# A two-layer Conformer trunk on one core: values product of the attention as two split passes, with a written matmul order, weight remainders by adding DMA and the residual parked in DRAM

## The chip, the cores and the metric

The kernel runs on one core of a Trainium2 chip. The metric is the device time of one execution in microseconds (us). Engines are named as the profile names them: PE is the matrix engine (PEld its weight loads), DVE the vector engine, ACT the activation engine, POOL the general engine, SP the engine that issues most DMAs.

## The reference

The input is 512 frames of 1024 channels; 16 learned meta tokens are put in front, which makes 528 tokens. Two layers follow, each with a feed-forward block (SwiGLU, 2816 wide, added at half weight), a mixer, and a second feed-forward block. A final norm drops the meta tokens.

The mixer normalises the stream to `u` and makes one combined projection into q, k, v (512 wide each), a convolution's value `a` and gate `b` (512 each), and two output gates `gs` and `gc` (1024 each). Branch A is stick-breaking attention, 8 heads of 64 channels: with z = q·k/8, the weight of an earlier token s for token t is sigmoid(z_ts) times the product of 1 − sigmoid(z_tj) over the tokens j between them. In logarithms that is a softplus, a running sum over the keys and an exponential. Branch B is a gated causal convolution of 31 taps, a LayerNorm and a swish. Each branch goes through a projection to 1024 (`ao`, `co`), is multiplied by the sigmoid of its gate, and their sum goes through `wo` and is added to the stream.

## The kernel before

**Number format.** The matrices are fp32. A fast pass of the PE takes operands in a shortened form (fp32r), so each factor is split into a rounded part `hi` and a remainder `lo`, and a product is three passes: hi·hi, hi·lo, lo·hi. `split` (L71) does it with an ACT copy (L73, the rounded part) and a DVE subtraction (L74, the remainder). Activations lie with channels on the partitions and tokens along the free dimension; in the last layer's mixer and second feed-forward block only the 512 frames are computed (mode `XO`), before that all 528 tokens (mode `FULL`, two halves of 264 columns).

**Weights.** `units` (L124) lists every weight tile in the order of use. For the mixer a unit is a 128 x 1024 tile (512 KB), for one output block of 128 channels. `fetch` (L171) brings raw tiles by DMAs on SP's queue into three buffers (`RAW`); `prep_unit` (L205) splits a raw tile into `wh` and `wl`, of which there are four buffers each; `unit` (L230) prepares up to `LOOK` = 3 units ahead of the one handed out. In the feed-forward blocks some sums of weight tiles are made by DMAs that add into SBUF, issued by POOL (`fetch_sums`, L202).

**The mixer** (L644) runs in stages. First the four `b` and `a` units, whose product becomes the convolution's input. Then, for each of four pairs of heads i, the projections q, k, v (`qkv`, L732) and `attend` (L749); some `gs` units follow each pair (`GS_FILL`). The attention of a pair cuts the keys into four blocks (`PIECES`, L642) with 256, 272, 400 and 512 query columns. For each block: scores q·k into PSUM (L816, L817) and the causal mask (L819); a softplus of three ACT passes and one DVE pass (L743); a split (L829); the running sums as products with triangular and all-ones matrices (L833 to L836); an exponential on ACT into `a` (L839); the values product (L843). That last product is in plain fp32, for each head on 64 of the array's 128 columns, the two heads' outputs on the two halves of one PSUM bank. An extra small fp32 product (L809) brings in the 16 last keys. After all keys `po` is split into `oh` and `ol` (L845).

The last stage (L857 on) multiplies the attention's output by `ao`, makes the eight `gc` units, ends the convolution (`conv_some`, L680, which otherwise puts four taps behind each evacuation on DVE), normalises it (`chan_sum` on POOL, L878; `rstd_from`, L902), multiplies by `co`, then `wo`, and adds to the residual `h`.

**Order.** A list scheduler puts each engine's instructions into a fixed order when the kernel is built, by priority. `attend` runs at raised priority and its values products at lowered priority (`priority(EARLY)`), so the attention's matmuls are strewn among the projections'. PSUM holds three `ps` banks for projections, two `z` tiles of two banks and one `po` bank during the attention.

Of the kernel before, what the change touches and what calls it, by code (L numbers as in the profile page):

```python
# [7 lines left out]
F32 = mybir.dt.float32  # L8
# [5 lines left out]
P = 128  # L14
# [20 lines left out]
GS_FILL = ((0,), (1,), (2,3), (4,5, 6, 7))  # L35
NEG = -1e30

# [18 lines left out]
def kernel(ctx, tc, hT, par, const, wg1, wu1, wd1, win, wao, wco, wout, wg2, wu2, wd2, out):  # L56
# [8 lines left out]
    spool = ctx.enter_context(tc.tile_pool(name="spool", bufs=1))  # L65

# [58 lines left out]
    for l in range(DEPTH):  # L125
        for fi, (wg, wu, wd) in enumerate(((wg1, wu1, wd1), (wg2, wu2, wd2))):
            if fi == 1:
                for i in range(4):
                    units += [(("b", l, i), win[l, 16 + i], 8), (("a", l, i), win[l, 12 + i], 8)]
                for i in range(4):  # L130
                    units += [(("q", l, i), win[l, i], 8), (("k", l, i), win[l, 4 + i], 8), (("v", l, i), win[l, 8 + i], 8)]
                    if i:
                        units += [(("gs", l, j), win[l, 20 + j], 8) for j in GS_FILL[i - 1]]
                units += [(("gs", l, j), win[l, 20 + j], 8) for j in GS_FILL[3]]
                units += [(("ao", l, jj), wao[l, jj], 8) for jj in range(4)]
                units += [(("gc", l, j), win[l, 28 + j], 8) for j in range(8)]
                units += [(("co", l, jj), wco[l, jj], 8) for jj in range(4)]
                units += [(("wo", l, j), wout[l, j], 8) for j in ORDER]
# [66 lines left out]
    def prep_unit():  # L205
# [47 lines left out]
    h = [hpool.tile([P, T], F32, name=f"h{k}") for k in range(KD)]  # L253
# [390 lines left out]
    def mixer(l, st, omode, after):  # L644
        last = omode == XO
        with ExitStack() as es:
            bp = es.enter_context(tc.tile_pool(name=f"mix{l}", bufs=1, reuse_waits="tile"))
            u = st["u"]
            rs = {}
            halves = {FULL: (slice(0, HALF), slice(HALF, T)), XO: (slice(META, T),)}  # L650
# [17 lines left out]
            def times(dst, outs, other, d0=0, taps=CONV_STEP):  # L668
# [3 lines left out]
                conv_some(taps, i)  # L672
# [24 lines left out]
            def project(psp, *key, mode=FULL):  # L697
                return gemm_b(psp, unit(*key), 0, KD, u, mode)

            with tc.tile_pool(name=f"psm{l}", bufs=3, space=bass.MemoryType.PSUM, reuse_waits="tile") as psp, \  # L700
# [6 lines left out]
                with tc.tile_pool(name=f"glu{l}", bufs=1, reuse_waits="tile") as glu:  # L707
                    for i in range(4):
                        outs = project(None, "b", l, i)
# [8 lines left out]
                        times(c, project(psp, "a", l, i), rs["r"], PAD)  # L718
# [3 lines left out]
                gates = []  # L722

                def gate_sb(j):
                    g = spool.tile([P, T], F32, tag="sa", bufs=8, name=f"gs{j}")
                    times(g, project(psp, "gs", l, j, mode=omode), rs["r"])
                    gates.append(g)

                o_parts = []
                with tc.tile_pool(name=f"att{l}", bufs=1, reuse_waits="tile") as ap_:  # L730

                    def qkv(i):  # L732
                        ts = []
                        for nm, s, mode in (("q", 0.125, omode), ("k", 1.0, FULL), ("v", 1.0, FULL)):
                            t = spool.tile([P, T], F32, tag="sb", bufs=4, name=nm + "f")
                            for ps, c in project(psp, nm, l, i, mode=mode):
                                ev = dve.scalar_tensor_tensor(out=t[:, c], in0=ps, scalar=s, in1=rs["r"][:, c],  # L737
                                                              op0=ALU.mult, op1=ALU.mult)
                            conv_some(CONV_STEP, ev)
                            ts.append(t)  # L740
                        return ts
# [7 lines left out]
                    def attend(i, qf, kf, vf):  # L749
                        QS, KH, KL = [], [], []  # L750
                        qc = META if last else 0
                        for hh in range(2):
                            r = slice(64 * hh, 64 * hh + 64)
                            o = slice(64 - 64 * hh, 128 - 64 * hh)
                            qs = ap_.tile([P, T], F32R, tag=f"qs{hh}", bufs=1, name="qs")
                            kh = ap_.tile([P, SEQ], F32R, tag=f"kh{hh}", bufs=1, name="kh")
                            kl = ap_.tile([P, SEQ], F32R, tag=f"kl{hh}", bufs=1, name="kl")
                            act.copy(qs[r, qc:], qf[r, qc:])
                            act.copy(kh[r], kf[r, :SEQ])
                            act.copy(kh[o], kf[r, :SEQ])  # L760
                            dve.tensor_tensor(out=qs[o, qc:], in0=qf[r, qc:], in1=f(qs[r, qc:]), op=ALU.subtract)
                            dve.tensor_tensor(out=kl[r], in0=kf[r, :SEQ], in1=f(kh[r]), op=ALU.subtract)
                            dve.tensor_tensor(out=kl[o], in0=kf[r, :SEQ], in1=f(kh[r]), op=ALU.subtract)
# [7 lines left out]
                        zs = ztile()[:, 0, :]  # L771
# [9 lines left out]
                        pe.matmul(zs[:, :w], l4[:, 0:P], e4[:, :w], start=False, stop=True, skip_group_check=True)  # L781
                        pe.matmul(zs[:, 32:48], l4[:, P:2 * P], e4[:, :16], start=True, stop=True, skip_group_check=True)
                        fn(a4[:, :w], zs[:64, :w], AF.Exp, bias=bias[:64, 3:4])
                        corner = ap_.tile([P, 2, 16], F32, tag="corner", bufs=2, name="corner")
                        zc = zs[96:128, 0:64].rearrange("p (a b) -> p a b", a=2)[:, :, :16]
                        dve.tensor_copy(corner[96:128], zc)

                        pt = psp.tile([P, 512], F32, tag="ps", name="pt")
                        for t in range(4):
                            pe.transpose(pt[:, t * P:(t + 1) * P], vf[:, t * P:(t + 1) * P], ident)  # L790
                        v = ap_.tile([P, 4, P], F32, tag="v", bufs=2, name="v")
                        dve.tensor_copy(v.rearrange("p t c -> p (t c)"), pt)
                        vb = ap_.tile([64, 2, P], F32, tag="vb", bufs=2, name="vb")
                        pool.memset(vb, 0.0)
                        pt = psp.tile([P, 512], F32, tag="ps", name="pt2")
                        pe.transpose(pt[:16, :P], vf[:, SEQ:T], ident)
                        for hh in range(2):
                            c = slice(64 * hh, 64 * hh + 64)
                            act.copy(vb[32 * hh:32 * hh + 16, 0, c], pt[:16, c])
                            if not last:  # L800
                                act.copy(vb[32 * hh:32 * hh + 16, 1, c], v[:16, 0, c])
                        oh = bp.tile([P, T], F32R, tag=f"oh{i}", bufs=1, name="oh")
                        ol = bp.tile([P, T], F32R, tag=f"ol{i}", bufs=1, name="ol")
                        if not last:
                            pe.matmul(zs[:, 64:80], vb[:, 1, :], a4[:, 16:32], start=True, stop=True, skip_group_check=True)
                            act.copy(oh[:, :META], zs[:, 64:80])
                            dve.tensor_tensor(out=ol[:, :META], in0=zs[:, 64:80], in1=f(oh[:, :META]), op=ALU.subtract)
                        po = psz.tile([P, 512], F32, tag="o", bufs=1, name="po")
                        pe.matmul(po[:, 496:512], vb[:, 0, :], a4[:, :16], start=True, stop=False, skip_group_check=True)  # L809
                        later = []  # L810
                        for t, q0, n, m0 in PIECES:
# [9 lines left out]
                            zz = z[:, :, :n]  # L821
                            sp = ap_.tile([P, 2, 512], F32, tag="big", bufs=4, name="sp")[:, :, :n]
# [184 lines left out]
```

## Time and profile before

| | us |
|---|---|
| median of 3 runs (2201.63 to 2203.7) | 2202.39 |
| the profiled execution, its own time | 2201.58 |
| span of the profiled execution, first to last instruction | 2199.8 |
| PE busy | 2181.2 |
| DVE busy | 1616.1 |
| ACT busy | 1034.7 |
| POOL busy | 386.2 |

Busy time is the union of an engine's instruction times, so overlapping matmuls count once. A matmul's recorded duration contains its way through the array, in which the next one already runs: what one matmul costs is the distance to the next start. The two mixers take about 369 to 753 us and 1470 to 1842 us of the span; the rest is feed-forward.

### The profile page before, as it was taken

How to read it: one execution, taken by the hardware profiler on the slowest of the kernel's cores; microseconds unless marked ns; L12 is line 12 of the kernel's file. 1: busy time of each engine (PE TensorE's matmuls, PEld its weight loads, DVE VectorE, ACT ScalarE, POOL GpSimd, SP SyncE). 2: the span in 40 equal slices, each digit the busy share in tenths (PEclk: the TensorE clock that was granted, in tenths of full speed). 3: DMA queues.
4: the chain of work that ended last, by engine and by line, in shares of the span. 5: the costliest groups of instructions: out<-in, count | busy, mean ns of one | idle time of the engine just before them, and what ended most of it. 6: DMA issues, size and time to landing. Idle time of an engine off the chain costs nothing.

```text
span 2199.8 us, 39441 instructions
## 1 busy us (share of the span) xinstructions
PE 2181.2 (99%) x16210; PEld 2060.7 (94%) x16210; DVE 1616.1 (73%) x2152; ACT 1034.7 (47%) x1454; POOL 386.2 (18%) x321
## 2 busy tenths in 40 slices
PE   9999999999999999999999999999999999999998
PEld 9999999988899999999999999999777788999897
DVE  7867686877787767676877676868777787776685
ACT  6434355366525435343554343553665265344354
POOL 1322310000000122313113223101000001312220
PEclk9999999999999999999999999999999999999999
DMA  8465443211122456464365654432111225575532
GB/s 232 140 158 142 127 116 106 87 49 52 55 87 87 135 135 172 139 164 122 97 168 151 162 141 129 115 106 87 56 41 68 86 96 139 155 181 139 154 105 78
DMA packets 120580, 261.68 MB, mean 119 GB/s; under 512 B 13392, under 2 KB 17488, under 8 KB 120400
## 3 DMA queue, kind: packets, MB, share of 16 engines
q1 hardware_dynamic: 97248, 217.70, 30.1%
q0 software_dynamic: 22464, 40.90, 11.5%
q8 instruction: 127, 2.08, 0.4%
q10 hardware_dynamic: 688, 0.55, 0.1%
q14 instruction: 53, 0.43, 0.1%
HBM read 257.01 MB, written 2.10 MB: 118 GB/s over the span
## 4 chain that ended last, share of the span: by engine, by line
PE 97%; DVE 1%; ACT 1%; issue 0%; POOL 0%; DMA 0%; POOLq 0%; DVEq 0%; ACTq 0%
PE ps L664 25%; PE ps L547 15%; PE pb L547 15%; PE ps L246 11%; PE pb L246 6%; PE pe L246 6%; PE pe L547 5%; PE z L664 2%; PE ps L474 2%; PE po L843 2%; PE pe L474 1%; PE z L833 1%; PE pb L474 1%; PE ps L521 1%; PE z L816 1%; PE z L835 1%
## 5 line engine op out<-in xcount | busy, mean ns | idle before, releaser
L73 ACT CAST wh<-wr 128x1024 fp32r<-128x1024 f32 (+4 forms) x379 | 352.5, 932 | 591.9 <-PE ps L664 168.3
L74 DVE TENSOR_TENSOR wl<-wr,wh 128x1024 fp32r<-128x1024 f32 (+4 forms) x379 | 438.7, 1159 | 71.9 <-ACT wh L73 66.4
L73 ACT CAST wh<-s 128x1024 fp32r<-128x1024 f32 x158 | 165.8, 1049 | 275.9 <-DVE s L223 91.3
L74 DVE TENSOR_TENSOR wl<-s,wh 128x1024 fp32r<-128x1024 f32 x158 | 215.9, 1366 | 59.5 <-ACT wh L73 58.8
L607 POOL TENSOR_TENSOR h<-h,dt 128x528 f32<-128x528 f32 (+1 forms) x96 | 179.2, 1872 | 261.2 <-DVE dt L605 258.4
L664 PE MATMUL ps<-uh,wh 128*128 128x264 f32 (+1 forms) x864 | 220.5, 312 | 0.3 <-DVE kf L737 0.3
L664 PE MATMUL ps<-uh,wl 128*128 128x264 f32 (+1 forms) x864 | 214.5, 308 | 0.0
L664 PE MATMUL ps<-ul,wh 128*128 128x264 f32 (+1 forms) x864 | 213.9, 307 | 0.0
L202 POOL DMA_DIRECT2D s<-wg x78 | 73.0, 945 | 746.2 <-DMA s<-wg 261.2
L692 DVE SCALAR_TENSOR_TENSOR y<-uc,prm,y 128x528 f32<-128x528 f32 (+1 forms) x240 | 181.4, 756 | 4.7
L547 PE MATMUL ps<-ul,wh 128*128 128x264 f32 (+1 forms) x624 | 177.3, 284 | 0.0
L547 PE MATMUL pb<-sl,wh 128*128 128x264 f32 (+1 forms) x624 | 176.9, 283 | 0.0
L547 PE MATMUL ps<-uh,wl 128*128 128x264 f32 (+1 forms) x624 | 176.8, 283 | 0.0
L547 PE MATMUL pb<-sh,wl 128*128 128x264 f32 (+1 forms) x624 | 176.8, 283 | 0.0
L547 PE MATMUL pb<-sh,wh 128*128 128x264 f32 (+1 forms) x624 | 176.5, 283 | 0.0
L547 PE MATMUL ps<-uh,wh 128*128 128x264 f32 (+1 forms) x624 | 176.1, 282 | 0.0
L664 PEld LDWEIGHTS ps<-uh,wh 128*128 128x128 f32 x864 | 143.2, 188 | 20.4 <-issue 10.7
L664 PEld LDWEIGHTS ps<-uh,wl 128*128 128x128 f32 x864 | 141.6, 188 | 13.4 <-issue 7.2
L664 PEld LDWEIGHTS ps<-ul,wh 128*128 128x128 f32 x864 | 142.0, 188 | 12.5 <-issue 6.6
L246 PE MATMUL ps<-al,wh 128*128 128x264 f32 (+1 forms) x616 | 142.4, 301 | 0.5 <-DVE al L74 0.2
L246 PE MATMUL ps<-ah,wh 128*128 128x264 f32 (+1 forms) x616 | 141.8, 300 | 0.0
L246 PE MATMUL ps<-ah,wl 128*128 128x264 f32 (+1 forms) x616 | 141.7, 300 | 0.0
(291 smaller groups left out, 5985.3 us busy)
## 6 DMA issues: line engine op xcount, KB each, us to landing
wr<-wd SPq DMA_DIRECT2D x96, 384.0 KB, 3.5
wr<-win SPq DMA_DIRECT2D x72, 512.0 KB, 3.2
wr<-wg SPq DMA_DIRECT2D x117, 256.0 KB, 3.0
wr<-wu SPq DMA_DIRECT2D x117, 256.0 KB, 3.4
s<-wg SPq DMA_DIRECT2D x78, 256.0 KB, 4.6
s<-wu SPq DMA_DIRECT2D x78, 256.0 KB, 5.9
s<-wg POOLq DMA_DIRECT2D x78, 256.0 KB, 5.2
s<-wu POOLq DMA_DIRECT2D x78, 256.0 KB, 7.1
```

Of the source, the lines that this page charges most:

```text
L73: act.copy(hi, x)
L74: dve.tensor_tensor(out=lo, in0=x, in1=f(hi), op=ALU.subtract)
L202: pool.dma_start(t[:, a:b], src, accum_op=ALU.add)
L246: pe.matmul(ps[:, c, :n], wt[:, k0 + k, :], xt[:, s:s + n], start=(k == 0 and pi == 0), stop=(k == nk - 1 and pi == 2))
L474: pe.matmul(ps[:, e, :TH], wt[:, k, :], xt[:, s], start=(k == ORDER[0] and pi == 0), stop=(k == ORDER[-1] and pi == 2))
L521: pe.matmul(ps[:, e, :TH], wt[:, k, :], xt[:, s], start=(k == 0 and pi == 0), stop=(k == KD - 1 and pi == 2))
L547: pe.matmul(ps[:, e, :TH], wt[:, 4 * e + kk, :], xt, start=start and kk == 0 and pi == 0, stop=kk == 3 and pi == 2, skip_group_check=True)
L607: pool.tensor_tensor(out=tri(h[j], mode), in0=tri(h[j], mode), in1=tri(t, mode), op=ALU.add)
L664: pe.matmul(ps, wt[:, k0 + k, :], xt[:, s], start=(n == 0 and pi == 0), stop=(n == nk - 1 and pi == 2))
L692: t = dve.scalar_tensor_tensor(out=y, in0=uc[i][:, c0 + k:k + T], scalar=col(w0 + k), in1=y, op0=ALU.mult, op1=ALU.add)
L816: pe.matmul(z[:, hh, :n], KH[hh][:, ks], qq, start=True, stop=False, skip_group_check=True)
L843: pe.matmul(po[c, q0 - META:q0 - META + n], v[:, t, c], a[:, hh, :], start=False, stop=(t == 0), skip_group_check=True)
```

## The change

- The values product: `a` is split into `ah` and `al`; the values of the two heads are laid out as [hi of head 0, lo of head 0, lo of head 1, hi of head 1], so that for one head the stationary tile is 128 columns wide and holds its hi and lo side by side. Two fp32r passes (`ah`, `al`) give the hi part and the lo part of the output on different halves of the partitions. `po` grows from one bank to two. `end` adds the halves: ACT copies of both, a DVE subtraction per head, and one DVE addition over the pair. The small product of the 16 last keys is issued once per head.
- The order: within the attention PE's instructions stand in the order in which the program writes them (`manual_schedule`). `attend` becomes a generator that yields nine or ten times per pair; at each yield half a projection (`by_halves`, one half of the tokens, or half the channels in mode XO) is issued. `products` lists q, k, v, gs and now four of the gc units for that. The tail of a pair (running sums of the longest block, the last values products, the end) is issued in three steps within the next pair. `ps` falls from three banks to two.
- Weights of the mixer: ACT writes `hi`, then ACT writes `−raw` into `lo` (which rounds to −hi), and a DMA issued by POOL adds the raw tile from DRAM a second time. The DVE subtraction is gone for these units.
- The residual: `h` is written to a DRAM tile by eight DMAs on SP at the mixer's start and read back by eight at the start of its last stage. In between its space holds qs, kh, kl and the temporary `ot`; `big` tiles go from four to six.
- The last stage: four gc units have moved ahead into the attention, `ao` stands after the convolution's sums, and `chan_sum` runs on DVE. The convolution takes two taps (three in mode XO) behind each half.

```diff
-GS_FILL = ((0,), (1,), (2,3), (4,5, 6, 7))
+GS_FILL = ((0, 1), (2, 3), (4, 5), (6, 7))
+GC_FILL = 4
+BIG = 6
+MIXER = ("b", "a", "q", "k", "v", "gs", "ao", "gc", "co", "wo")
...
-            split(raw[:, :nk], hi[:, :nk], lo[:, :nk])
+            if key[0] in MIXER:
+                act.copy(hi[:, :nk], raw[:, :nk])
+                act.activation(lo[:, :nk], raw[:, :nk], AF.Copy, scale=-1.0)
+                pool.dma_start(lo[:, :nk], src[:, :nk].bitcast(F32R), accum_op=ALU.add)
+            else:
+                split(raw[:, :nk], hi[:, :nk], lo[:, :nk])
...
+            keep = dram.tile([KD, P, T], F32, tag="keep", bufs=1, name="keep")
+            for k in ORDER:
+                nc.sync.dma_start(keep[k], h[k])
...
+                        v = ap_.tile([P, 4, 4, 64], F32R, tag="v", bufs=2, name="v")
+                        act.copy(v[:, :, 0:4:3], ptv)
+                        dve.tensor_tensor(out=v[:, :, 1:3], in0=ptv, in1=f(v[:, :, 0:4:3]), op=ALU.subtract)
...
-                                    pe.matmul(po[c, q0 - META:q0 - META + n], v[:, t, c], a[:, hh, :], start=False,
-                                              stop=(t == 0), skip_group_check=True)
+                            split(a, ah, al)
...
+                        def values(t):
+                            ah, al, q0, n = acts.pop(t)
+                            for hh in range(2):
+                                for p in (ah, al):
+                                    pe.matmul(po[:, hh, q0 - META:q0 - META + n], v[:, t, hh * P:hh * P + P], p[:, hh, :],
+                                              start=False, stop=(t == 0 and p is al), skip_group_check=True)
...
+                        def end():
+                            values(0)
+                            ot = hold(6, SEQ, "ot")
+                            for hh in range(2):
+                                r, o = (slice(64 * e, 64 * e + 64) for e in (hh, 1 - hh))
+                                act.copy(oh[r, META:], po[r, hh, :])
+                                act.copy(ot[r], po[o, hh, :])
+                                dve.tensor_tensor(out=ol[r, META:], in0=po[r, hh, :], in1=f(oh[r, META:]), op=ALU.subtract)
+                            dve.tensor_tensor(out=ol[:, META:], in0=f(ol[:, META:]), in1=f(ot), op=ALU.add)
+                        ends.extend((end, lambda: values(1), lambda: sums_and_weights(0)))
...
+                    with tc.manual_schedule(engines={mybir.EngineType.PE}):
+                        for i in range(4):
+                            for _ in attend(i, step, *parts(i)):
+                                next(beside, None)
...
+                for k in ORDER:
+                    h[k] = hpool.tile([P, T], F32, tag=f"h{k}", bufs=1, name=f"h{k}")
+                    nc.sync.dma_start(h[k], keep[k])
```

The order of a pair, as `attend` writes it ("|" is a yield, at which half a projection is issued): transposes of v and the corner product | running sums of the previous pair's longest block | its values(1) and scores(3) | its values(0) and end, small products | scores(2) | sums(3) | scores(1) | values(3), sums(2) | sums(1), scores(0) | values(2) |. The numbers are key blocks; block 3 has 256 query columns, block 0 has 512.

## Rows read from the trace of the kernel before

**Rows 1.** The page: the span, the busy time of PE, and the shares of the chain of waits by engine; then the head of the chain's own view, its shares by line.
```profile
span 2199.8 us, 39441 instructions
PE 2181.2 (99%) x16210; PEld 2060.7 (94%) x16210; DVE 1616.1 (73%) x2152; ACT 1034.7 (47%) x1454; POOL 386.2 (18%) x321
...
PE 97%; DVE 1%; ACT 1%; issue 0%; POOL 0%; DMA 0%; POOLq 0%; DVEq 0%; ACTq 0%
...
by line: PE ps L664 25.1%; PE ps L547 15.4%; PE pb L547 14.9%; PE ps L246 10.5%; PE pb L246 5.6%; PE pe L246 5.6%; PE pe L547 5.2%; PE z L664 2.2%; PE ps L474 2.1%; PE po L843 1.8%; PE pe L474 1.3%; PE z L833 1.2%; PE pb L474 1.1%; PE ps L5
```
**Rows 2.** Stretches of the span: attention (with the begin of the last stage) and the rest of the last stage of the first mixer. Columns: busy us of each engine with the number of instructions, granted clock, DMA share, GB/s.
```profile
404.00:665.00 261.00, 259.75 (x1908) 231.66 (x1907) 201.09 (x299) 132.43 (x192) 12.42 (x12) 1.00 0.19 63
665.00:753.00 88.00, 88.00 (x721) 87.94 (x720) 69.90 (x115) 50.45 (x73) 0.00 (x0) 1.00 0.27 90
```
**Rows 3.** The chain of waits in order of time (start us, us, what): one projection of 48 matmuls of 264 columns, and a run of 144 matmuls of 512 columns.
```profile
375.32 5.84 PE ps L664 x48
...
1707.06 33.45 PE ps L664 x144
```
**Rows 4.** PE's instructions in order of time, first mixer, around one values product (start us, us to the last end, line, operation, count).
```profile
448.91 0.28 PE L664 MATMUL ps<-ul,wh 128*128 128x264 f32 x1
449.12 0.65 PE L843 MATMUL po<-a,v 128*64 128x256 f32 x2
449.70 0.50 PE L816 MATMUL z<-qs,kh 128*128 128x512 f32 x1
450.03 0.39 PE L817 MATMUL z<-qs,kl 128*128 128x512 f32 x1
```
**Rows 5.** The same view of the second mixer, where the products of both heads stand together.
```profile
1578.22 1.08 PE L843 MATMUL po<-a,v 128*64 128x512 f32 x4
1579.23 0.51 PE L664 MATMUL ps<-uh,wh 128*128 128x512 f32 x1
```
**Rows 6.** Groups of PE's instructions by line and shape (count, busy us, mean ns of one, idle before).
```profile
L843 PE MATMUL po<-a,v 128*64 128x512 f32 x32 | 11.8, 618 | 0.0
L835 PE MATMUL z<-sh,trir 128*128 128x512 f32 x16 | 6.3, 395 | 0.0
L809 PE MATMUL po<-a,vb 64*128 64x16 f32 x16 | 3.0, 264 | 0.2 <-DVE ol L74 0.2
```
**Rows 7.** Groups on ACT and DVE in the first mixer's attention (404 to 665 us), by shape.
```profile
L73 ACT CAST wh<-wr 128x1024 fp32r<-128x1024 f32 x32 | 33.5, 1048 | 68.8 <-PE ps L664 60.7 <-PE z L664 5.1 <-issue 2.8
L97 ACT ACTIVATE sp<-sp,bias 128x800 f32<-128x800 f32 x8 | 7.7, 965 | 0.2
L744 ACT ACTIVATE sp<-z 128x800 f32<-128x800 f32 x4 | 3.3, 831 | 0.0
L73 ACT CAST sh<-sp 128x800 fp32r<-128x800 f32 x4 | 3.4, 859 | 1.4 <-DVE sp L747 1.4
L73 ACT CAST oh<-po 128x512 fp32r<-128x512 f32 x4 | 2.3, 585 | 2.3 <-PE po L843 2.3
...
L692 DVE SCALAR_TENSOR_TENSOR y<-uc,prm,y 128x528 f32<-128x528 f32 x109 | 83.3, 764 | 2.0
L74 DVE TENSOR_TENSOR wl<-wr,wh 128x1024 fp32r<-128x1024 f32 x31 | 41.7, 1345 | 1.1 <-ACT wh L73 0.8
L670 DVE TENSOR_TENSOR gs<-ps,rstd 128x264 f32<-128x264 f32 x16 | 6.4, 428 | 12.5 <-PE ps L664 12.5
L747 DVE SCALAR_TENSOR_TENSOR sp<-z,sp 128x800 f32<-128x800 f32 x4 | 3.9, 986 | 2.9 <-ACT sp L97 2.9
L74 DVE TENSOR_TENSOR sl<-sp,sh 128x800 fp32r<-128x800 f32 x4 | 4.0, 989 | 0.1
L74 DVE TENSOR_TENSOR ol<-po,oh 128x512 fp32r<-128x512 f32 x4 | 2.8, 692 | 3.4 <-ACT oh L73 3.4
```
**Rows 8.** Groups over the whole span: the split of a block's scores, all sizes together (rounded part, remainder).
```profile
L74 DVE TENSOR_TENSOR sl<-sp,sh 128x512 fp32r<-128x512 f32 (+3 forms) x32 | 29.0, 905 | 6.8 <-ACT sh L73 4.4 <-PE po L843 2.1
...
L73 ACT CAST sh<-sp 128x512 fp32r<-128x512 f32 (+3 forms) x32 | 25.4, 794 | 24.4 <-DVE sp L747 13.7 <-DVE sp L827 8.7 <-PE po L843 2.0
```
**Rows 9.** Who waited for whom over the span (total us, times, longest us): ACT's weight copies for a free buffer, and PE's waits in the attention.
```profile
ACT wh L73 <- PE ps L664: 168.3, 64, 6.9
...
PE pt L790 <- DVE vf L737: 2.2, 4, 0.7
```
**Rows 10.** DMA: the queues of SP and of POOL (packets, MB, share of 16 engines); one of the lines that issue on POOL's queue with KB each and median us to landing; POOL's adding DMAs alone, how long POOL was busy with one (ns, min, median, max) and the time to landing.
```profile
q1 hardware_dynamic: 97248, 217.70, 30.1%
q0 software_dynamic: 22464, 40.90, 11.5%
...
s<-wu POOLq DMA_DIRECT2D x78, 256.0 KB, 7.1
...
L202 POOL DMA_DIRECT2D s<-wu x78: 857/1192/2583, 28.8 to 2111.6; - x78
...
DMA to landing us min/median/max: 4.0/5.9/10.5
```
**Rows 11.** DVE in order of time at the end of the first mixer's convolution: from the norm to the first and the last split of its output.
```profile
666.65 0.70 DVE L378 TENSOR_SCALAR nt<-ps_ln 128x528 f32<-128x528 f32 x1
...
674.76 1.33 DVE L74 TENSOR_TENSOR yl<-y,yh 128x528 fp32r<-128x528 f32 x2 [0.53 <-ACT yh L73]
...
678.83 0.70 DVE L74 TENSOR_TENSOR yl<-y,yh 128x528 fp32r<-128x528 f32 x1
```

More of the change, by code (lines that the diff above doesn't have):

```diff
@@ L666, in gemm_b, with by_halves, times @@
                 return outs
-            def times(dst, outs, other, d0=0, taps=CONV_STEP):
+            def by_halves(psp, mode, *key):
+                hi, lo = unit(*key)
+                for s in halves[mode]:
+                    ps = psp.tile([P, 512], F32, tag="ps", name="ps")[:, :s.stop - s.start]
+                    for n, k in enumerate(ORDER):
+                        if n == KD // 2 and len(halves[mode]) == 1:
+                            yield None
+                        xh, xl = u[k]
+                        for pi, (wt, xt) in enumerate(((hi, xh), (hi, xl), (lo, xh))):
+                            pe.matmul(ps, wt[:, k, :], xt[:, s], start=(n == 0 and pi == 0),
+                                      stop=(n == KD - 1 and pi == 2))
+                    yield ps, s
+            def times(dst, outs, other, d0=0):
                 for ps, s in outs:
@@ L803, in attend @@
[L803 to L808, printed above, removed]
@@ L809, in attend @@
-                        pe.matmul(po[:, 496:512], vb[:, 0, :], a4[:, :16], start=True, stop=False, skip_group_check=True)
-                        later = []
-                        for t, q0, n, m0 in PIECES:
+                                act.copy(vb[32 * hh:32 * hh + 16, 2, c], pt[:16, c])
+                        yield
+                        step(0)
+                        if i:
+                            yield
+                        step(1)
+                        later, acts = {}, {}
@@ new lines, in attend @@
+                        dve.tensor_copy(corner[96:128], zc)
+                        scores(*PIECES[0])
+                        yield
+                        step(2)
+                        oh = bp.tile([P, T], F32R, tag=f"oh{i}", bufs=1, name="oh")
+                        ol = bp.tile([P, T], F32R, tag=f"ol{i}", bufs=1, name="ol")
+                        if not last:
+                            pe.matmul(zs[:, 64:80], vb[:, 2, :], a4[:, 16:32], start=True, stop=True, skip_group_check=True)
+                            with priority(-EARLY):
+                                act.copy(oh[:, :META], zs[:, 64:80])
+                                dve.tensor_tensor(out=ol[:, :META], in0=zs[:, 64:80], in1=f(oh[:, :META]),
+                                                  op=ALU.subtract)
@@ new lines, in attend @@
+                        yield
+                        scores(*PIECES[1])
+                        yield
+                        sums_and_weights(3)
+                        yield
+                        scores(*PIECES[2])
+                        yield
+                        po = psz.tile([P, 2, 512], F32, tag="o", bufs=1, name="po")
+                        for hh in range(2):
+                            pe.matmul(po[:, hh, 496:512], vb[:, hh, :], a4[:, :16], start=True, stop=False,
+                                      skip_group_check=True)
```

190 lines of the change are left out of this document (105 added, 85 removed).

## The prediction

> **What bounds the kernel now.** I read the page first: PE is busy for 2181.2 of the 2199.8 us of the span, and the chain of waits gives it 97% [rows 1]. So a change moves the time by what it takes off PE's row of work, or by the waits that it puts into that row. The stretches come next: in the attentions and in the last stage of the mixer PE is busy practically all the time as well, while DVE has 201 of 261 us and ACT 132 [rows 2]. A busy PE is not yet a PE at its pace, because overlapping durations hide small gaps. The pace stands in the chain in order of time: 48 matmuls of 264 columns in 5.84 us and 144 of 512 in 33.45 us, so 122 ns and 232 ns each, 0.455 ns a column [rows 3]. The list of who waited for whom shows no large wait of PE in the attentions; the largest, for the transposes, is 2.2 us in all [rows 9]. What remains is the price of the matmuls themselves, and there the fp32 values product stands out: 1.8% of the span lies on it [rows 1], that is 39.6 us.
>
> The profiled execution took 2201.58 us for a span of 2199.8, so 1.8 us lie around the span, and it is 0.8 us under the median of 2202.39. I make the sum in the trace and give the result against the median. A measurement of this kernel can tell about 0.2% (4.4 us) from no change.
>
> **The values product.** One product of 256 columns is two PE instructions, which hold PE from 449.12 to 449.70 us, 0.58 us [rows 4]; for 512 columns it is 1.01 us [rows 5]. After the change one head of one pair has 256+272+400+512 = 1440 columns in two passes, and there are 16 such heads in the two layers: 46,080 columns. Other fp32r products with the same 512 columns have the duration of the projections [rows 6], so I take 0.455 ns: 21.0 us. Saved: 39.6 − 21.0 = 18.6 us.
>
> The Trainium skill's page "TensorE: Matmul & The Clock Gate" (Part 3, packing small matmuls) says that products whose outputs lie in different column groups of the array run at the same time; the two heads of the old product are such a pair. The trace agrees where they stand next to each other: four instructions of 512 columns end together after 1.01 us [rows 5]. By that rule for all 64 products the old cost would be 24 us and the saving 3 us. The chain's 39.6 us is measured and decides: most of the 64 are not side by side.
>
> **Changing between formats.** Before a product the next start comes after 0.21 instead of 0.12 us (448.79, 448.91, 449.12), and after it the first matmul takes 0.33 instead of 0.23 (449.70, 450.03, 450.26) [rows 4]: 0.19 us for each burst of fp32. With 64 products, some of them neighbours, there are 32 to 64 bursts, 6 to 12 us; I take 56, 10.6 us, because the share on the chain says that most stand alone. This goes wholly, since the new passes have the format of the projections around them.
>
> **The small product of the last keys** is issued twice per pair instead of once: 16 more instructions. The 16 of before are busy 3.0 us [rows 6]. Cost 0 to 3.0 us, taken as 3.0, because short fp32 work doesn't hide behind its neighbours.
>
> So PE's own work falls by 18.6 + 10.6 − 3.0 = 26.2 us. The rest of the change must not hand that back.
>
> **Load of DVE and ACT.** In the first attention's 261 us DVE loses 31 remainders, 41.7 us [rows 7]; it gains 16 remainders of `a` at 0.905 (the price of the same tiles of the scores [rows 8]), 14.5 us, and three subtractions or additions instead of one at a pair's end, 4 x 2 x 0.69 = 5.5 us. That makes 201 − 42 + 20 = 179 us. ACT gains the negated copies (33.5 us as the rounded ones [rows 7]), 16 copies of `a` at 0.794 [rows 8] = 12.7 us, three more copies per pair's end at 0.585 [rows 7] = 7.0 us, and the four copies of v that it takes over at that price, 2.3 us: 132 + 55.5 = 188 us. In a stretch of some 248 us that is 72% and 76%. Neither becomes the bound, so I cost the work at nothing; but in queues so full a waiting chain meets other work.
>
> **The written order.** PE executes in order, so a matmul that waits holds all that follows. The tightest place is block 1 with 400 query columns: after its scores, two half projections (2 x 2.92), values(3) (4 x 0.12) and sums(2) (about 8 x 0.12) are written before sums(1) needs its softplus: 7.3 us. The softplus with its split takes 0.83 + 2 x 0.965 + 0.99 + 0.86 + 0.99 = 5.6 us unhindered [rows 7]. The 1.7 us between are used up by one convolution tap (0.76) and one weight copy (1.05) ahead in the queues [rows 7]. The other blocks have three half projections and more. I charge one such tap, 0.75 us, for each of the eight pairs: 6 us. The bounds are nothing (the cover holds everywhere) and, at the other end, a wait at each of the 39 yields per layer, which is the rival below. PSUM banks for projections fall from three to two: a half takes 2.9 us and its evacuation about 0.43, so DVE may be some 2.5 us late before PE notices; that too is in the 6 us.
>
> **Remainders by adding DMA.** A weight tile's buffers come free when the unit four places earlier ends (ACT's copies wait for exactly that, 168.3 us in all [rows 9]), and the tile is wanted three units later: 3 x 5.84 = 17.5 us in the last stage, more in the attention. Of this ACT takes 2 x 1.05 and POOL about 1.2 for the issue, which leaves some 14 us to land. The adding DMAs of 256 KB landed in 5.2 and 7.1 us (the second of a pair) and 10.5 at most [rows 10]; 512 KB is bounded by 5.2 below and twice 10.5 above, and I take 8, near a pair's 7.1, which is the same bytes. The engines bear it: SP's queue took 30.1% of the span for 217.7 MB, 1.6 us per 512 KB, POOL's 11.5% for 40.9 MB, 3.2 us [rows 10], together 4.8 of 5.84 us per unit in the last stage. I cost it at nothing; its cover is the lead of three units, and if that goes, every late microsecond is one of PE's.
>
> **The residual, the sums, the other moves.** Writing and reading h is 2.2 MB each way, 6.6 us of the DMA engines at SP's rate [rows 10]. On SP's queue the reads stand ahead of later weight fetches and wait for the last pair's end, some 5 us of copies; raw tiles are fetched about three units ahead, so this takes 12 of 17 us of lead and costs nothing by itself. Six channel sums per layer on DVE cost 0.7 us each, in a stage where DVE also loses its remainders. After the norm's matmul the convolution's first output took 8.8 us and its last 12.9 [rows 11]; the two gc units that are left to cover it last 11.7 us, and the first is wanted first. Nothing, at most 2 us per layer. What is late next is then the same row of matmuls.
>
> The sum: 2201.6 − 26.2 + 6 = 2181.4 in the trace, **2182 us** for the median.
>
> **Rivals.**
> *The written order starves PE (slower).* If the queues of ACT and DVE are so ordered that at each of the 78 yields the awaited tile is 0.5 us late, PE stands for 39 us: 2202.4 − 26 + 39 = 2215. It decides from 0.34 us per yield on. For it: both queues above 70%, chains of six hops between the two engines, and two ps banks. Against it: most blocks have 9 us or more of cover for chains of 4 to 7 us. Chance 0.11.
> *Remainders land late (slower).* Were 512 KB to take 15 us instead of 8, each of the 20 or so units of a last stage would be about 1 us late, 40 us in all: 2216. It decides from about 14 us. For it: 83% of the DMA engines in that stage. Against: 10.5 us as the longest of 156. Chance 0.04.
> *The heads already run side by side.* Saving 3 and 32 bursts (6), less 3 and the waits of 6: 2202. Against it stands the chain's 39.6 us. Chance 0.02; with waits that happen to eat the whole gain, 0.07 within 0.2%.
> *The order costs nothing and closes other gaps.* All 64 bursts (12 us) go, and the transposes' waits: 18.6 + 12 + 2 and little for the small products: 2170. Chance 0.13.
> My forecast, 2174 to 2196, has 0.65.
>
> **The numbers.** Faster: 0.65 + 0.13 = 0.78; the same 0.07; slower 0.11 + 0.04 = 0.15. The range goes from 2167 (just under the best case) to 2208, which leaves out most of the two slow cases, about 0.13, and a few hundredths below.
>
> **What would show it.** Right: line 843's group is replaced by 128 fp32r matmuls on 128 x 128 whose share of the chain is near 1%, and the attentions shorten by about 10 us each. The written order is the culprit if the list of waits shows PE waiting for ACT or DVE tiles of the softplus (sh, sl, a) or for evacuations; the remainders are, if PE waits for a DMA of wl. My forecast is wrong if the other stages move, for they hold none of the terms.

## The result, and the profile after

The changed kernel takes **2171.4 us** (median of 4, 2171.02 to 2172.01) against 2202.35 on the same chip: ratio 0.9859, 95% interval [0.9842, 0.9876], so 31 us faster. The forecast was 2182, with a range of 2167 to 2208. The profiled execution took 2171.02 us.

The page: PE is still busy for all but 19 us of the span [rows 1].
```profile
span 2169.2 us, 39870 instructions
...
PE 2149.9 (99%) x16226; PEld 2067.0 (95%) x16226; DVE 1533.6 (71%) x2108; ACT 1171.8 (54%) x1622; POOL 461.0 (21%) x413
```
Stretches of the first mixer, columns as in [rows 2]: its attention and its last stage. From its first `b` matmul to the first matmul after it the mixer took 384.9 us before and 370.3 after, the second one 371.2 and 356.8: 29.0 of the 30.6 us by which the span is shorter.
```profile
404.00:630.00 226.00, 224.60 (x1763) 215.53 (x1762) 173.52 (x274) 172.86 (x246) 28.73 (x34) 1.00 0.62 138
630.00:735.00 105.00, 104.82 (x853) 104.48 (x852) 65.97 (x123) 68.96 (x94) 12.97 (x15) 1.00 0.73 167
```
PE in order of time around one block's values product, which answers to [rows 4, 5]: the four passes of a block start 0.12 us apart, as projections do. The two heads' 256 columns take 0.58 us from 459.11 to 459.69, of which 0.11 is the first one's delay behind the fp32 products of L920; in [rows 4] one head alone took 0.58.
```profile
458.57 0.61 PE L920 MATMUL po<-a,vb 64*128 64x16 f32 x4
459.11 0.39 PE L891 MATMUL po<-ah,v 128*128 128x256 f32 x1
459.34 0.28 PE L891 MATMUL po<-al,v 128*128 128x256 f32 x1
459.45 0.28 PE L891 MATMUL po<-ah,v 128*128 128x256 f32 x1
459.57 0.28 PE L891 MATMUL po<-al,v 128*128 128x256 f32 x1
459.69 0.28 PE L876 MATMUL z<-sh,onesm 128*128 128x256 f32 x1
```
The groups [rows 6], and who waited for whom on PE [rows 9]. The waits for `sl`, `yh` and `vb` are the mixers' whole price in waits, 3.2 us; the one at L532 is a feed-forward's.
```profile
L891 PE MATMUL po<-ah,v 128*128 128x512 f32 x16 | 6.3, 393 | 0.0
L891 PE MATMUL po<-al,v 128*128 128x512 f32 x16 | 6.3, 393 | 0.0
L920 PE MATMUL po<-a,vb 64*128 64x16 f32 x32 | 4.9, 264 | 0.0
```
```profile
PE ps L532 <- ACT wh L77: 4.9, 1, 4.9
PE z L879 <- DVE sl L78: 1.9, 2, 1.0
...
PE ps L683 <- ACT yh L77: 0.9, 2, 0.7
...
PE z L894 <- ACT vb L843: 0.4, 1, 0.4
```
ACT and DVE in the attention [rows 7]: the copies of weights are now twice on ACT, and the remainders of weights are gone from DVE.
```profile
L223 ACT ACTIVATE wl<-wr 128x1024 fp32r<-128x1024 f32 x29 | 30.6, 1055 | 0.0
...
L940 DVE TENSOR_TENSOR ol<-po,oh 64x512 fp32r<-64x512 f32 x8 | 5.5, 687 | 2.7 <-ACT ot L939 2.6
...
L78 DVE TENSOR_TENSOR al<-a,ah 128x1024 fp32r<-128x1024 f32 x4 | 4.9, 1224 | 3.7 <-ACT ah L77 3.0 <-PE ps L697 0.7
```
DMA [rows 10]: the queues; the adding DMAs of `win` (KB each, median us to landing); h on its way to DRAM and back; the line that issues the adding DMAs, with its landing times.
```profile
q1 hardware_dynamic: 101856, 226.36, 32.8%
q0 software_dynamic: 37440, 95.44, 25.9%
...
wl<-win POOLq DMA_DIRECT2D x72, 512.0 KB, 7.7
...
keep<-h SPq DMA_DIRECT2D x16, 264.0 KB, 3.4
h<-keep SPq DMA_DIRECT2D x16, 264.0 KB, 7.3
...
L224 POOL DMA_DIRECT2D wl<-win x72: 856/861/883, 356.5 to 1721.0; - x72
...
DMA to landing us min/median/max: 5.7/7.7/9.9
```
**A ledger of PE.** Busy time doesn't show what a group costs, so I summed, for every matmul of the two mixers, the distance from its start to the next one's. It counts what the next one waited as well. Values are in us, from the profiled execution of each kernel; "heads adjacent", "fp32 pair, list order" and "low parts last" are experiments 1, 5 and 11 below. The norms' own products, 3.7 us before and 3.8 after, are left out:

| | before | heads adjacent | fp32 pair, list order | changed | low parts last |
|---|---|---|---|---|---|
| projections (4128) | 620.1 | 618.2 | 610.3 | 607.9 | 607.9 |
| values product | 40.5 | 24.2 | 23.9 | 22.7 | 22.7 |
| running sums | 48.5 | 49.0 | 47.1 | 50.0 | 46.6 |
| scores | 23.2 | 24.0 | 21.9 | 21.9 | 21.9 |
| masks | 5.2 | 4.4 | 4.2 | 4.3 | 4.3 |
| small products (the last keys', transposes, corners) | 14.9 | 14.8 | 14.7 | 16.5 | 16.5 |

From before to changed: values −17.8, projections −12.2, scores −1.3, masks −0.9, sums +1.5, small products +1.6, norms +0.1: −29.0, as the two stretches have it.

### The profile page after: what moved, and what is told of

Same layout as the page of the kernel before. It is cut to its first block, busy times and chain, and to the rows that moved or that the text cites. A ratio compares the mean times of both kernels' runs of the same rounds, so it can differ in the third digit from the quotient of the medians.

```text
span 2169.2 us, 39870 instructions
## 1 busy us (share of the span) xinstructions
PE 2149.9 (99%) x16226; PEld 2067.0 (95%) x16226; DVE 1533.6 (71%) x2108; ACT 1171.8 (54%) x1622; POOL 461.0 (21%) x413
## 5 line engine op out<-in xcount | busy, mean ns | idle before, releaser
L77 ACT CAST wh<-wr 128x1024 fp32r<-128x1024 f32 (+4 forms) x275 | 243.9, 890 | 377.1 <-PE ps L257 93.4
L78 DVE TENSOR_TENSOR wl<-wr,wh 128x1024 fp32r<-128x1024 f32 (+4 forms) x275 | 300.1, 1094 | 60.1 <-ACT wh L77 56.2
L697 PE MATMUL ps<-uh,wh 128*128 128x264 f32 (+1 forms) x768 | 236.6, 308 | 0.0
L697 PE MATMUL ps<-ul,wh 128*128 128x264 f32 (+1 forms) x768 | 232.3, 302 | 0.0
L697 PE MATMUL ps<-uh,wl 128*128 128x264 f32 (+1 forms) x768 | 232.2, 302 | 0.0
L725 DVE SCALAR_TENSOR_TENSOR y<-uc,prm,y 128x528 f32<-128x528 f32 (+1 forms) x240 | 186.0, 775 | 4.2
L222 ACT CAST wh<-wr 128x1024 fp32r<-128x1024 f32 x104 | 109.3, 1051 | 128.7 <-issue 41.1
L558 PE MATMUL ps<-ul,wh 128*128 128x264 f32 (+1 forms) x624 | 177.4, 284 | 0.0
L558 PE MATMUL ps<-uh,wl 128*128 128x264 f32 (+1 forms) x624 | 176.8, 283 | 0.0
L558 PE MATMUL ps<-uh,wh 128*128 128x264 f32 (+1 forms) x624 | 176.3, 282 | 0.0
L224 POOL DMA_DIRECT2D wl<-win x72 | 62.2, 864 | 430.2 <-ACT wl L223 326.7
```

Of the source, the lines that this page charges most:

```text
L77: act.copy(hi, x)
L78: dve.tensor_tensor(out=lo, in0=x, in1=f(hi), op=ALU.subtract)
L222: act.copy(hi[:, :nk], raw[:, :nk])
L224: pool.dma_start(lo[:, :nk], src[:, :nk].bitcast(F32R), accum_op=ALU.add)
L558: pe.matmul(ps[:, e, :TH], wt[:, 4 * e + kk, :], xt, start=start and kk == 0 and pi == 0, stop=kk == 3 and pi == 2, skip_group_check=True)
L697: pe.matmul(ps, wt[:, k, :], xt[:, s], start=(n == 0 and pi == 0), stop=(n == KD - 1 and pi == 2))
```

## The experiments

All are compared with the kernel before on the same chip (2201.07, 2202.04 and 2201.94 us in the three sets).

**1. Heads side by side in the old kernel.** Theory: two passes of the full array save the 18 us. Rival: the old product was dear only because the planner put other matmuls between the two heads. In the old order 8 of the 32 blocks had both heads together.
```diff
-                            with priority(EARLY):
+                            with priority(0):
```


> The kernel before with one word changed: the values products are no longer issued at lowered priority, so in PE's order the two heads' fp32 products of all 32 blocks stand next to each other (8 of 32 did before). Theory side by side (heads in different columns of the array overlap): the products fall from 40 to about 24 us on PE and the bursts of fp32 from 56 to 32, 24 x 0.19 = 4.6 us; together some 20 us, 2181 to 2184 us. Theory serial (the overlap in the second mixer was an accident of the records): only the bursts, 2197 to 2200. Rival order (the low priority kept PE from waiting for the exponential): new waits, 2200 or more.

Measured 2183.0, ratio 0.9916 [0.9901, 0.9931]. All 32 blocks are together now. PE in order of time: four fp32 instructions of 256 columns, 0.58 us for both heads.
```profile
442.46 0.65 PE L843 MATMUL po<-a,v 128*64 128x256 f32 x4
443.04 0.23 PE L819 MATMUL z<-maskb,identb 128*128 128x128 bf16 x1
```
Taken singly, the two heads' instructions start 0.007 us apart (442.457 and 442.464, then 442.724 and 442.731), so they run at the same time. One word changed gives 18 us of the 31; the product fell from 40.5 to 24.2 us in its old format.

**2. The changed kernel with the old product, heads side by side**, and with it the single small product and the plain split of `po`.
```diff
-                            split(a, ah, al)
-                            acts[t] = (ah, al, q0, n)
+                            acts[t] = (a, q0, n)
...
-                                for p in (ah, al):
-                                    pe.matmul(po[:, hh, ...], v[:, t, hh * P:hh * P + P], p[:, hh, :],
+                                c = slice(64 * hh, 64 * hh + 64)
+                                pe.matmul(po[c, 0, ...], v[:, t, c], a[:, hh, :],
```


> The changed kernel with the old arithmetic of the values product: plain fp32 on 64 columns per head, the heads next to each other in the written order, one small product per pair, no split of a and no adding of halves. Theory format and passes: 24 us for the products if the heads overlap, against 22.7 measured, plus 32 bursts x 0.19 = 6 us, less 2 us for the small products: about 2177. If the heads do not overlap: 48 us, about 2200. Rival load (ACT and DVE hold PE up in the changed kernel; here they have 50 us less to do): not slower than 2172.

Measured 2170.39, ratio 0.9859 [0.9843, 0.9875]: the changed kernel's time without the split passes. They save 1.2 us of the product (23.9 to 22.7) and 2.5 at the projections, where the changes of format beside the product are gone (610.4 to 607.9). They give back 2.9 in the running sums (47.1 to 50.0), which wait for `sl`, and 1.8 in the small products. The expectation had 2177. Its 6 us for changes of format were too many, because in the written order only 35 projections stand next to these products, 22 ahead and 13 behind; and it didn't have the running sums.

**3. As 2, but each head on all 128 columns** (both heads' values, of which one half is used), so that the heads cannot share the array.
```diff
-                                pe.matmul(po[c, 0, ...], v[:, t, c], a[:, hh, :],
+                                pe.matmul(po[:, hh, ...], v[:, t, :], a[:, hh, :],
```


> The changed kernel with plain fp32 values products whose stationary tile is both heads' values, 128 columns, so that two products can never share the array (each gives an unused half). Same count of fp32 instructions and bursts as with 64 columns. Theory side by side: 48 us instead of 24 for the 64-column pair, so 24 us over that kernel, about 2201 to 2203. Rival (width makes no difference, heads ran one after the other anyway): the same time as the 64-column pair within 2 us.

Measured 2184.27, ratio 0.9924 [0.9909, 0.9938], 13.9 us over experiment 2. The product costs 35.3 instead of 23.9 us, in the same place and format: two heads one behind the other hold PE 0.78 us for 256 columns. Most of the rest of the difference is the second small product, 1.8 us. The expectation had 24 us over experiment 2, by twice the time for each product; 0.78 isn't twice the 0.58 of experiment 1. The wider tile itself isn't slower: its instructions start 0.22 us apart (458.95, 459.16, 459.38), those of a lone head in the kernel before 0.27 (449.12, 449.39).
```profile
458.63 1.13 PE L884 MATMUL po<-a,v 128*128 128x256 f32 x4
459.41 0.47 PE L873 MATMUL z<-sh,onesm 128*128 128x256 f32 x1
```
So what the chip gives for standing side by side is 11 us of product here; in the old kernel 16. Why it was 5 us more there wasn't tried; a lone head also stood between two other formats.

**4, 5. The order: planned by priority instead of written**, in the changed kernel and in that of experiment 2.
```diff
-                    with tc.manual_schedule(engines={mybir.EngineType.PE}):
+                    with priority(0):
```


> The changed kernel without the manual schedule: the list scheduler orders PE too, with the program's order as priority. Theory work (the gain is in PE's work, not in the order): within 5 us of the changed kernel, 2169 to 2177. Rival order (written order removes strewn matmuls and waits): 10 us or more slower, 2181 and up.

> The fp32-pair kernel (changed kernel, old arithmetic of the values product, heads adjacent) without the manual schedule, so the list scheduler orders PE. In the changed kernel the list order cost 14.6 us, of which its trace shows 12.7 as PE waiting for the split of a, which this kernel doesn't have. Theory waits (the written order is worth what the split of a would make PE wait): within 3 us of the fp32-pair kernel, 2169 to 2174. Rival strewing (the written order is worth it because it keeps the attention's matmuls together): 2180 or more, as the kernel before with adjacent heads (2183).

With split passes 2185.98, ratio 0.993 [0.9915, 0.9945]; with the fp32 pair 2170.61, ratio 0.9857 [0.9842, 0.9871]. So the written order is worth 14.6 us beside the split passes and nothing without them: what counts is whether a values product has to wait for one more hop, the copy `ah`. By starts the planner's order has 15.7 us more in the values product and 1.7 more in the projections, and 2.5 less in the running sums. And the fp32 pair in the planner's order is as fast as the changed kernel: the split passes and the written order are not what its gain needs. Once per layer the planner puts the eight sigmoids of the gates, and a table load, in front of that copy on ACT; in experiment 5 the sigmoids stand in the same place, and no product waits behind them. Whether moving the sigmoids alone would do as well as the written order wasn't tried. The waits of PE, ACT in order of time, and the stretches around the wait (columns as in [rows 2]):
```profile
PE po L891 <- ACT ah L77: 11.8, 2, 5.9
```
```profile
611.43 4.38 ACT L101 ACTIVATE gs<-gs 128x528 f32<-128x528 f32 x8
...
617.73 1.28 ACT L97 ACT_TABLE_LOAD   x1
619.02 1.04 ACT L77 CAST ah<-a 128x1024 fp32r<-128x1024 f32 x1
```
```profile
614.00:620.00 6.00, 0.23 (x2) 0.00 (x0) 1.41 (x2) 5.97 (x8) 0.86 (x1) 0.94 0.28 74
620.00:626.00 6.00, 5.42 (x19) 4.62 (x20) 1.91 (x2) 2.23 (x5) 0.00 (x0) 0.50 0.62 117
626.00:632.00 6.00, 6.00 (x51) 6.00 (x51) 3.15 (x6) 2.08 (x3) 0.00 (x0) 1.00 0.17 45
```
Read the granted clock, the last but two: after the idle time PE works for 6 us at 0.50, that is 1.2 of 2.4 GHz. So a wait of 5.9 us costs about 3 more in what follows; after the second one the half speed lasted 4.4 us.

**6, 7. Remainders of the mixer's weights on DVE**, without adding DMAs, in the kernel of experiment 2 and in the changed one.
```diff
-MIXER = ("b", "a", "q", "k", "v", "gs", "ao", "gc", "co", "wo")
+MIXER = ()
```


> The fp32-pair kernel with the mixer's weight remainders subtracted on DVE as before (no adding DMA, no negated copy on ACT). Theory PE bound (DVE and ACT have room): within 2 us of the fp32-pair kernel, 2169 to 2173. Rival DVE relief (31 remainders of 1.3 us in an attention, 42 us, make the evacuations or the softplus late for a written order): 2178 or more.

> The changed kernel with the mixer's weight remainders on DVE (no adding DMA), split values product kept. DVE then has 174 + 42 - 0 = 215 us of work in the first attention's 226 us. Theory PE bound: 2171 to 2176. Rival DVE relief: DVE becomes the bound of the attention or makes the split of a late: 2185 or more, and the list of waits shows PE waiting for DVE.

2178.26, ratio 0.9892 [0.9877, 0.9907], and 2183.47, ratio 0.9915 [0.99, 0.993]: 7.9 and 12.1 us dearer. In both, the norm at the convolution's end comes late in the second mixer: eleven remainders of 1.22 us stand among the convolution's last taps on DVE from 1650 us on, and in experiment 6 the last tap ends at 1729.8 us instead of 1723.4 in experiment 2. The waits in experiment 7, and PE behind the first of them in experiment 6, where it is the same:
```profile
PE ps L683 <- ACT yh L77: 5.4, 1, 5.4
...
PE z L879 <- DVE sl L78: 4.0, 7, 1.4
```
```profile
1747.96 0.80 PE L683 MATMUL ps<-yh,wh 128*128 128x512 f32 x1 [5.38 <-ACT yh L77]
...
1749.70 0.63 PE L683 MATMUL ps<-yh,wh 128*128 128x512 f32 x1
...
1753.65 0.39 PE L683 MATMUL ps<-yh,wh 128*128 128x512 f32 x1
```
512 columns start 0.43 us apart (1749.70, 1750.13) until 1753.65, then 0.23: 5.7 us at half speed, 2.8 lost. 5.4 + 2.8 = 8.2, where 7.9 were measured. The other 4 of experiment 7 stand in the running sums (54.2 against 50.0 us): the waits for `sl` grow from 1.9 to 4.0, one of 1.0 for `sh` comes in, and behind two waits of 1.0 and 1.4 us, 0.5 us of work apart, the granted clock was 0.50 for 3.4 us. DVE is busy for 205 of 226 us in the first attention and 175 of 205 in the second, where all of this stands.

**8. The lead of the weights, two units instead of three**, in the changed kernel.
```diff
+            if units[state["prep"]][0][0] in MIXER and state["prep"] > state["use"] + 2:
+                break
```


> The changed kernel with the mixer's weights prepared two units ahead of the one in use instead of three. The adding DMA of 512 KB landed in 7.7 us (median, 9.9 at most), ACT takes 2.1 and POOL 0.9 before it: 10.7 us of a lead of 11.7 in the last stage. Theory lead (the cover is the lead in units): on the edge, 0 to 1 us late at some of 40 units, 2171 to 2190. Rival (the buffers, not the lead, set the start of the copies): no change.

2179.38, ratio 0.9897 [0.9881, 0.9914]: 8 us dearer. The wait that I had named as this step's failure is there; landing took 6.1 to 11.8 us. Behind the longer wait 3.0 us at a granted clock of 0.50 follow, 1.5 lost: with the waits that is 7.3 of the 8.
```profile
PE ps L685 <- DMA wl<-wco: 5.8, 2, 4.7
```
**9. Experiment 1 with the adding DMAs.**
```diff
-            split(raw[:, :nk], hi[:, :nk], lo[:, :nk])
+            if key[0] in MIXER:
+                act.copy(hi[:, :nk], raw[:, :nk])
+                act.activation(lo[:, :nk], raw[:, :nk], AF.Copy, scale=-1.0)
+                pool.dma_start(lo[:, :nk], src[:, :nk].bitcast(F32R), accum_op=ALU.add)
...
```


> The kernel before with two edits: the two heads' values products stand side by side in the order (which alone took 2183.0 us), and the mixers' weight remainders are made by an ACT copy of -raw and an adding DMA instead of a DVE subtraction, as in the changed kernel. What is open: of the 31 us the adjacency of the heads has about 19, and some 12.6 us are shared by the written order with halves and the adding DMA. Theory A (the adding DMA is worth something only as relief of DVE where the written order makes PE wait for DVE's chain; in the planner's order PE hardly waits): 2181 to 2185, no difference from 2183.0. Theory B (the remainders on DVE cost the same 8 us in any order, by the norm's chain in the last stage): 2173 to 2177. Theory C (in the old order, where POOL also makes the channel sums of the last stage and 87 us of half the mixer's chains, the adding DMAs are issued late): above 2188.

2181.28, ratio 0.9906 [0.9892, 0.9919]: 1.7 us under experiment 1, overlapping intervals. Relief of DVE is worth what DVE's lateness costs PE, and in the old order that was almost nothing.

**10. Masks and identity in fp32r instead of bf16**, in the kernel of experiment 2.
```diff
-    identb = cst.tile([P, P], BF16, name="identb")
-    maskb = cst.tile([P, 240], BF16, name="maskb")
+    identb = cst.tile([P, P], F32R, name="identb")
+    maskb = cst.tile([P, 240], F32R, name="maskb")
...
```


> The changed kernel with the values product as in the fp32 pair (2170.39 us there) and, new, the identity and the two causal masks with their right factors in fp32r instead of bf16, so that the mask products have the format of the scores around them. Theory A (each change of format costs about 0.09 us before and 0.10 us after a burst): 32 bursts of bf16 and their returns fall away, 32 x 0.1 to 32 x 0.19 = 3 to 6 us: 2164 to 2168. Theory B (only fp32, not bf16, pays for a change of format, because the gap belongs to fp32's passes): 2170 to 2171. Theory C (short fp32r products cost more than bf16 ones of the same columns): 2172 or more.

2172.92, ratio 0.9867 [0.9853, 0.988]: nothing gained. The return from bf16 does cost, but the bf16 masks are as much shorter. Two masks and the first two projections behind them, first in experiment 2, then here:
```profile
441.23 0.38 PE L856 MATMUL z<-maskb,identb 128*128 128x240 bf16 x2
441.37 0.37 PE L697 MATMUL ps<-uh,wh 128*128 128x264 f32 x1
441.57 0.28 PE L697 MATMUL ps<-ul,wh 128*128 128x264 f32 x1
```
```profile
441.40 0.38 PE L856 MATMUL z<-maskb,identb 128*128 128x240 f32 x2
441.62 0.29 PE L697 MATMUL ps<-uh,wh 128*128 128x264 f32 x1
441.75 0.28 PE L697 MATMUL ps<-ul,wh 128*128 128x264 f32 x1
```
Two masks hold PE for 0.14 us in bf16 and 0.22 in fp32r; after the 32 bursts of bf16 the first projection is longer by 0.085 us in the mean, after those of fp32r by 0.041. Up to the second projection the two take 0.34 and 0.35 us. Over all the masks are 2.4 us dearer in fp32r, the projections behind them 1.4 cheaper.

**11. Low parts last.** The two waits for `sl` stand at the longest block of a layer's last pair, where nothing is written between the products with `sh` and with `sl`. Here the second head's products with `sh` come first.
```diff
                                 pe.matmul(z[:, hh, :n], trir, sh[:, hh, :], start=False, stop=False, skip_group_check=True)
+                            for hh in range(2):
                                 pe.matmul(z[:, hh, :n], trir, sl[:, hh, :], start=False, stop=True, skip_group_check=True)
```


> The changed kernel with the running sums reordered within a step: the products with the rounded part sh of both heads first, those with the remainder sl of both heads after them, so that a late sl is hidden behind one more head's products. Theory A (the waits of PE for sl, 1.9 us in all, and the half clock that may follow one, are what the written order costs): 2168 to 2170. Theory B (these waits are covered already or turn into waits for sh): 2171 to 2172, no difference.

**2167.66**, ratio 0.9844 [0.9831, 0.9858], 3.7 us under the changed kernel and the best of all here. PE there, first in the changed kernel, then in this one:
```profile
606.44 0.50 PE L878 MATMUL z<-sh,trir 128*128 128x512 f32 x1
607.98 0.50 PE L879 MATMUL z<-sl,trir 128*128 128x512 f32 x1 [1.04 <-DVE sl L78]
```
```profile
607.35 0.40 PE L878 MATMUL z<-sh,trir 128*128 128x512 f32 x1
607.73 0.74 PE L880 MATMUL z<-sl,trir 128*128 128x512 f32 x2
```
No wait for `sl` is left in the list, and the running sums fall from 50.0 to 46.6 us in the ledger: the whole gain. Of these 3.4 us, 2.2 stand at the two blocks of the waits and 1.2 at five other longest blocks, 0.2 to 0.3 us each, which the list of waits doesn't name. The intervals of the two ratios overlap; that the gain is real rests on the ledger. With it the split passes come to 2.7 us less than the fp32 pair, from another set of runs and with overlapping intervals too.

## Why the prediction was right, and what it misread

It was right in sign and range for the reason it gave: PE's row of work is the time, and the change takes the lone fp32 products and their format changes out of it. The time lies below its own band of 2174 to 2196, though, and the mixers shortened by 14.6 and 14.4 us where it had about 10 for each attention. By its steps:

- **Values product**, forecast 39.6 to 21.0: 40.5 to 22.7, −17.8. The size holds, the attribution does not. The prediction weighed the Trainium skill's rule (page "TensorE: Matmul & The Clock Gate", Part 3) that products in different column groups run at the same time, and let the chain's 39.6 us decide against it. That was right for the order before, and experiments 1 to 3 show the rule at work as soon as the heads are neighbours: 24.2 us where it gave 24. The two passes by themselves bring 1.2 us. The same gain comes from taking away the distance between two instructions.
- **Format changes**, forecast 10.6 us. Beside a lone fp32 burst in the trace of before, the projection ahead is longer by 0.091 us in the mean (39 of them) and the one behind by 0.106 (45): 0.197 for each burst, where the text had 0.19. Summed, that is about 9 of the 12.2 us that the projections lose. Two rows of that reading, and the landing time of 5.2 us, are not among the groups shown ahead; they are, from PE in order of time and the DMA issues of before:
```profile
448.79 0.28 PE L664 MATMUL ps<-uh,wh 128*128 128x264 f32 x1
...
450.26 0.39 PE L816 MATMUL z<-qs,kh 128*128 128x512 f32 x1
```
```profile
s<-wg POOLq DMA_DIRECT2D x78, 256.0 KB, 5.2
```
- **Small product**, forecast +3.0: +1.9 by starts (2.5 to 4.4). The 16 of before hold PE for 2.5 of the 3.0 us that they are busy, so a part of such a product does lie beside its neighbours.
- **The written order**, forecast +6: the mis-sized term. The sums are dearer by 1.5 us only, the waits for `sl` among them (by experiment 11 these cost 3.4, and the sums of before were 1.9 dearer than with the low parts last). The waits stand where the text had not looked, in the last pair, at the longest block. Block 1, which it called the tightest, never waited. Nor did the two `ps` banks show.
- **Gains not in the sum**: scores −1.3, masks −0.9, some 3 us of the projections (half of it waits ahead of the transposes, which are gone) and 1.6 outside the mixers. This and the 4.5 us less for the order are what puts 2171.4 beside the rival "the order costs nothing and closes other gaps" (2170), the nearest case. Its number is met in part by luck: its bursts gave 9 us and not 12, the order wasn't free, and 3.8 us (scores, masks, outside the mixers) had a term nowhere. The difference between experiments 9 and 5 shows that 10.7 us come with what is left of the change: the new order of the program with its halves and moved units, the parked residual and the channel sums on DVE. Which of these gives how much was not tried, and the cause of this third of the gain stays open. It has no single place: from experiment 1 to 2 the largest pieces in the projections are 2.6 us ahead of running sums, 1.9 behind small products and 1.6 ahead of transposes.
- **Load and adding DMA**, costed at nothing, right with the cover named: DVE 173.5 and ACT 172.9 of 226 us (forecast 179 and 188 of 248), landing in 7.7 us (forecast 8). With one unit of lead less the cover is gone at two places (experiment 8). On DVE instead the remainders cost 8 to 12 us in the new order, which the text had not priced.
- **Residual and sums**: h leaves in 3.4 us and returns in 7.3, and no wait of PE names these DMAs; one of 0.5 us for the sum in `h` on DVE, behind the first mixer, is new. The norm's wait is 0.9 us in all, where at most 2 per layer were allowed.

The rivals "starves PE" and "remainders land late" did not come; experiments 4, 7 and 8 are kernels in which their mechanisms do, at two to eleven places per run instead of 78.

## To other kernels

Before a costly product is rewritten, see in PE's order of time whether the instructions that could share the array stand next to each other; one priority may give most of the gain. A change that adds a hop in front of a matmul (a copy, a split) needs an order in which that matmul stands late enough; judge both together, because here the order alone was worth nothing and the hop alone cost 15 us. And where a high and a low part are multiplied, try the low parts of all heads last; here that gave 3.4 us of PE's time.

## What the runs showed of the hardware that was not expected

A single idle time of PE of 4.7 to 5.9 us was followed by 3 to 6 us at a granted clock of 0.50 (experiments 4, 6, 7 and 8), so it cost some 6 to 9 us. A wait of 1.0 us in the changed kernel was followed by none, but two of 1.0 and 1.4 us close together were followed by 3.4 us (experiment 7). The masks' formats were a surprise too: by starts a bf16 product of 240 columns holds PE for 0.07 us and an fp32r one for 0.11, and the projection behind the bf16 ones is later by about as much as they save.
